# Small tiles padded so that every tile TensorE reads begins at the same place modulo 256 bytes

## The chip, the core and the metric

The kernel runs on one core of a Trainium2 chip. The core has a matrix engine (TensorE; PE in the profile, PEld for its weight loads), a vector engine (VectorE, DVE), an activation engine (ScalarE, ACT), GpSimd (POOL) and SyncE (SP, which here issues the weight DMAs). They share SBUF, a memory of 128 partitions, and run on their own, held together by semaphores; TensorE reads SBUF and writes its sums to PSUM. The metric is the device time of one launch in microseconds: the median of three runs is 2596.28 us (2596.21 to 2597.89).

## The reference

Two small transformers in a row, over 512 tokens of 1024 features, all in float32. The first has a latent attention, a squared-ReLU feed-forward, a differential attention and a second such feed-forward, each followed by a layer norm of `alpha * x + m`. The second has a forgetting attention, a SwiGLU, a retention and a second SwiGLU, each behind an RMS norm and added to `x`.

```python
def first_block(x, ...):
    for i in range(2):
        m = _mla(x, ...) if i == 0 else _diff_attn(x, ...)
        x = _layernorm(ALPHA * x + m, ln_mix_g[i], ln_mix_b[i])
        x = _layernorm(ALPHA * x + square(relu(x @ ffn_w_up[i])) @ ffn_w_down[i],
                       ln_ffn_g[i], ln_ffn_b[i])
    return x

def second_block(x, ...):
    for i in range(2):
        h = rmsnorm(x, norm_mix[i])
        x = x + (forgetting_attention(h, ...) if i == 0 else retention(h, ...))
        h = rmsnorm(x, norm_ffn[i])
        gu = h @ ffn_w_in[i]
        x = x + (silu(gu[..., :D_FF_2]) * gu[..., D_FF_2:]) @ ffn_w_out[i]
    return rmsnorm(x, final_norm)
```

The feed-forwards are 1024 to 4096 to 1024 in the first block and 1024 to 2 x 2816, then 2816 to 1024, in the second.

## The kernel before

Everything stays in SBUF: the stream `X` as four tiles of 128 tokens by 1024 features, and its transpose, features on partitions, in two parts `XH` and `XL`. float32 products are made of float32r ones: each operand is split into a high part and what is left of it (`split`, lines 113 to 120: ScalarE rounds, VectorE subtracts), and each product is three matmuls, high by high, high by low and low by high (`mm3`, lines 148 to 153; lines 150, 151 and 152 are the three). Weights come from HBM in chunks of 512 KB (128 partitions by 1024 numbers) into the two tiles `raw`, and are split into the rings `whi` and `wlo` of five tiles each.

There are eight stages: `mla`, `f0`, `diff`, `f1`, `fox`, `g0`, `ret`, `g1` (four attentions, each followed by its feed-forward). Two forms of product carry nearly all the time:

- `fgemm` (line 160): a 128-column piece of the weights is the stationary operand, the one that TensorE loads ahead; `XH` or `XL` with 512 tokens is the moving one, streamed through. In the profile these are `ps<-XH,whi` and so on (the projections in the up half of a feed-forward, the gates of the retention) and `pj<-XH,whi` (query and key projections). The first four tiles behind a norm run in halves of 256 tokens (`fhead`, line 168).
- `mm_t` (line 204): 128 tokens of the activations are stationary, 512 columns of the weights move. These are `ta`, `tb<-whi,jh` (the down half of a feed-forward, whose hidden activations `h` or `z` are split into `jh` and `jl` just ahead), `v<-whi,XH` (values) and `ta`, `tb<-whi,VH` (output projections).

TensorE loads the stationary operand of the next matmul while the present one streams, so two reads of SBUF run beside each other. Attention scores of one query tile (`s`), the softmax on the other engines, the transposes of its result (`pt`) and the product with the values (`o`) are woven into projections that fill TensorE's time: `PLAN` says how many filler products go with a query tile (`n`), and how much of TensorE's work in ns (`ln`, `sm`, `pv`, ...) is put before something that waits for a chain of the other engines. That work is counted in `tick` (line 131) as columns at 2.4 GHz, not measured.

SBUF is given out by pools, one after the other; a tile begins where the tile ahead of it ends, rounded up to 32 bytes per partition. So a small tile moves the begin of all that lie behind it. The places of the built program, modulo 256 bytes, are these (all matmul operands are cut from their tiles in steps of 512 or 2048 bytes, so a cut has its tile's place; the one exception is the 32-column weight of the forget gates):

| tiles | before | with the change |
|---|---|---|
| `X`, `XH`, `XL`, `idn` (the identity), `mask` | 128 | 128 |
| `raw`, `whi`, `wlo`, all stages | 224 | 128 |
| `CH`, `KH`, `qkh`, `PH` and their low parts in `mla` | 224 | 128 |
| `jh`, `jl` in `f0`, `f1`; `VH`, `VL` in `diff`, `fox` | 224 | 128 |
| `jh`, `jl` in `g0`, `g1`; all operands of `ret` (`H`, `L`, `VH`, `AH`, `zj`, `jh`, `yn`) | 96 | 128 |
| `qa`, `ka`, `kl` in `diff` | 64 | 128 |
| `PH`, `PL`, `e0`, `e1`, `sq` in `diff` | 160 | 128 |
| `qkh`, `qkl`, `ck`, `ch`, `PH`, `PL`, `e` in `fox` | 192 | 128 |

The tiles that cause this are `mh` (4 numbers) and `col` (16), line 55; the 24 small tiles of line 71; `ss` in `rms_fin` (2 numbers, four of them, line 345); `nlam`, `sub` and `ones` in `diff` (line 736); `s1` there (4 numbers, three buffers, line 793); and `bf` and `rc` in `fox` (line 856). A program prints the functions:

Of the kernel before, what the change touches and what calls it, by code (L numbers as in the profile page):

```python
# [9 lines left out]
F32 = mybir.dt.float32  # L10
# [5 lines left out]
PSUM = bass.MemoryType.PSUM  # L16
# [3 lines left out]
NT = 4  # L20
# [8 lines left out]
AUTO = True  # L29
# how much of the tensor engine's other work (ns) is put before what waits for a chain of the  # L30
# other engines, and how many products of that work go with each query tile
PLAN = {
# [8 lines left out]
class Net:  # L41
    def __init__(self, ctx, tc, A):
        self.tc, self.nc, self.A = tc, tc.nc, A
        nc = self.nc
        self.cst = ctx.enter_context(tc.tile_pool(name="cst", bufs=1))
        self.wp = ctx.enter_context(tc.tile_pool(name="wp", bufs=1))
        self.sm = ctx.enter_context(tc.tile_pool(name="sm", bufs=1))
        self.pp = ctx.enter_context(tc.tile_pool(name="pp", bufs=8, space=PSUM))
        c = self.cst
        self.X = c.tile([128, NT, D], F32, name="X")  # L50
        self.XH = c.tile([128, 8, S], F32R, name="XH")
        self.XL = c.tile([128, 8, S], F32R, name="XL")
        self.idn = c.tile([128, 128], F32, name="idn")
        self.mask = c.tile([128, S], F32, name="mask")
        self.mh = c.tile([128, 4], F32, name="mh")
        self.col = c.tile([128, 16], F32, name="col")
        self.seq = []
        self.n_dma = self.n_split = self.n_get = self.n_done = 0
        self.raw, self.sp = {}, {}
        self.fq = []  # L60
        self.unit = 0
        self.rt = self.tables = None
        self.late = {}
        self.owed = 0
        self.clk, self.dq, self.busy = 0.0, [], False
# [4 lines left out]
    def small(self, n, name):  # L70
        return self.sm.tile([128, 8], F32, tag="small", name=name, bufs=24)[:, 0:n]

    # weight stream: every chunk is [128, n] of float32, split into two float32r parts
    def dma_next(self, eng=None):
# [46 lines left out]

    # work behind a chain of the other engines is issued only after enough of the tensor
    # engine's other work: clk counts what the tensor engine was given, in ns
    def defer(self, delay, fn):
# [33 lines left out]

    # features on partitions: out[m, tok] over kts k-tiles, weights stationary
    def fgemm(self, ps, w, off, kts, xh, xl, n0=0, n1=S, m=128):  # L160
# [5 lines left out]

    # the first tiles after a norm run in token halves, so that the norm's tail is hidden
    def fhead(self, n, evac):
# [35 lines left out]
    def mm_t(self, ps, t, lh, ll, w, first, last):  # L204
        # two k-tiles of a [128 tok, 512] product
        ts = slice(t * 128, t * 128 + 128)
        for j in range(2):
            ws = slice(j * 512, j * 512 + 512)
            self.mm3(ps, lh[:, j, ts], ll[:, j, ts], w[0][:, ws], w[1][:, ws], first and j == 0, last and j == 1)

    # tokens on partitions: out[tok, 1024] in two column halves, lhs(c) -> (hi, lo) [128, 2, 512]
    def t_first(self, nch, lhs, fin0, ahead=True):
# [69 lines left out]

    # one 512-column half of a normed [128, 1024] token tile into xT
    def to_xT(self, src, t, g):
# [56 lines left out]
    def rms_fin(self, pool, g, dst=None):  # L341
        nc = self.nc
        X = [self.halves(self.X[:, t, :]) for t in range(NT)]
        G = self.halves(g)
        ss = [pool.tile([128, 2], F32, name=f"ss{t}", bufs=1) for t in range(NT)]
        out = {}

        def add(t, h, ps):
            nc.vector.tensor_tensor(X[t][h], X[t][h], ps, op=ALU.add)
            tmp = pool.tile([128, 512], F32, tag="ntmp", name="ntmp", bufs=self.plan.get("nb", 4))  # L350
            nc.scalar.activation(tmp, X[t][h], AF.Square, accum_out=ss[t][:, h:h + 1])

        def a(t, ps):
            add(t, 1, ps)
            rs = self.rms_scale(ss[t], D)
            for h in range(2):
                tmp = pool.tile([128, 512], F32, tag="ntmp", name="nt2", bufs=self.plan.get("nb", 4))
                nc.vector.scalar_tensor_tensor(tmp, X[t][h], rs, G[h], op0=ALU.mult, op1=ALU.mult)
                if dst is not None:
                    nc.sync.dma_start(out=dst[t * 128:t * 128 + 128, h * 512:h * 512 + 512], in_=tmp)  # L360
                out[t, h] = tmp

        def fb(t):
            for h in range(2):
                self.to_xT(out.pop((t, h)), t, h)

        return lambda t, ps: add(t, 0, ps), a, (fb if dst is None else lambda t: None), True
# [10 lines left out]

    # causal softmax numerators of [128 q, keys] in PSUM; sum into rs
    def softmax(self, pool, s, qt, tag, sm, scale=1.0):  # L380
# [22 lines left out]

    # out^T [dv, q] = sum over keys of V^T P^T; V is [tok, head, (tile, dv)], and the result takes
    # the place of its head's values as [dv, head, (tile, q)]
    def pv(self, VH, VL, h, PH, PL):
# [6 lines left out]

    # heads cut into query tiles: scores of one tile, other work for the tensor engine, and the
    # transposes and values behind the chains of the softmax
    def attend(self, pool, heads, scores, VH, VL, post, fills):
# [25 lines left out]

    # rotary embedding with features on partitions; swap names, in each group of 32 partitions, the
    # partner of a feature
    def rope(self, pool, src, swap, C, Sn):
# [8 lines left out]

    # cos and signed sin of positions * inv, features on partitions
    def rope_tables(self, pool, tmp, which, tags=("t0", "t1", "t2"), bufs=1):
# [212 lines left out]

    # attention, its output projection and the norm behind it  # L670
    def attn_out(self, outer, p, scores, VH, VL, nready, post, fills, gname, bname, row):
# [42 lines left out]

    # one 512-column half of a token-major projection: 4 chunks of two k-tiles
    def v_half(self, VH, VL, dst):
# [11 lines left out]
    def diff(self):  # L728
        nc, A, tc = self.nc, self.A, self.tc
        mm = nc.tensor.matmul  # L730
        with ExitStack() as outer:
# [3 lines left out]
            p = outer.enter_context(tc.tile_pool(name="d_a", bufs=1))  # L735
            nlam = p.tile([128, 1], F32, name="nlam")
            sub = p.tile([128, 1], F32, name="sub")
            ones = p.tile([128, 2], F32, name="ones")
            with tc.tile_pool(name="d_0", bufs=1) as p0:
# [15 lines left out]
            p = outer.enter_context(tc.tile_pool(name="d_b", bufs=1))  # L755
            qk, ready, s1 = {}, set(), {}

            def evac(h, which):
                def f(ps):
                    r = self.rope(p, ps, DIFF_SWAP, C, Sn)  # L760
                    # a sub-head's queries lie above their low parts, its keys twice: one product of full
                    # height gives two of the three parts
                    if which == 0:
                        qk[h] = [p.tile([128, 2, S], F32R, tag=n, name=n, bufs=2) for n in ("qa", "ka")]
                        qk[h].append(p.tile([128, S], F32R, tag="kl", name="kl", bufs=2))
                    q, k, kl = qk[h]
                    for i in range(2):
                        own, other = slice(64 * i, 64 * i + 64), slice(64 - 64 * i, 128 - 64 * i)
# [19 lines left out]
            def scores(h, qt):  # L788
# [3 lines left out]
                if qt == 0:  # L792
                    s1[h] = p.tile([128, 4], F32, tag="s1", name="s1", bufs=3)
                q, k, kl = qk[h]
                ss = [self.ps("s") for _ in range(2)]
# [17 lines left out]
            def post(h, o):  # L813
# [6 lines left out]
                def sums():  # L820
# [5 lines left out]
                    nc.vector.tensor_copy(s8, sps[:, 0:8])  # L826
                    # the values lack the division by the sum of the first softmax; so does eps
                    nc.vector.tensor_tensor(rr, s1[h], s1[h], op=ALU.mult)
# [19 lines left out]
    def fox(self):  # L848
        nc, A, tc = self.nc, self.A, self.tc
        mm = nc.tensor.matmul  # L850
        with ExitStack() as outer:
# [3 lines left out]
            pa = p = outer.enter_context(tc.tile_pool(name="x_a", bufs=1))  # L855
            bf = p.tile([32, 1], F32, name="bf")
            nc.gpsimd.dma_start(out=bf, in_=A["fox_b"])
            rc = p.tile([32, 16], F32, name="rc")
            nc.gpsimd.dma_start(out=rc, in_=A["c_rows"])
# [282 lines left out]
def pack_v(w):  # L1142
    # 512 columns, two k-tiles a chunk
    return w.reshape(-1, 2, 128, 512).transpose(0, 2, 1, 3).reshape(-1, 128, 1024)


def pack_h(w):
    # two 512-column halves, each in chunks of two k-tiles
    return np.concatenate([pack_v(np.ascontiguousarray(w[:, :512])), pack_v(np.ascontiguousarray(w[:, 512:]))])


# rotary features of the latent attention, the two halves side by side in each group of 32
ROPE_ORDER = np.array([16 * (i // 32) + i % 16 + 32 * (i % 32 // 16) for i in range(64)])
# [110 lines left out]
```

## Time and profile before

| | |
|---|---|
| median of three runs | 2596.28 us (2596.21 to 2597.89) |
| profiled execution, first to last instruction | 2594.1 us |
| outside that span, against the median | 2.2 us |
| TensorE busy, granted clock | 2561.4 us (99%), 0.998 of full speed |
| VectorE, ScalarE, GpSimd busy | 1289.7 us (50%), 929.4 us (36%), 170.4 us (7%) |
| DMA | 233.05 MB, mean 90 GB/s |

Matmuls are pipelined: the profile models each one's end, so that its shown duration (some 390 ns at 512 columns) overlaps the next. What counts for the time is the pitch, the distance from one matmul's start to the next one's start. It is read from the start times of a timeline, or from a row that gives the first and the last start and the count of a group.

### The profile page before, as it was taken

Reading aid. Unit: us, or ns where it says so; the run is one execution under the profiler, and the core shown is the slowest. Engines: PE = TensorE matmul, PEld = TensorE weight load, DVE = VectorE, ACT = ScalarE, POOL = GpSimd, SP = SyncE. Lnnn points to the kernel's source line nnn. Section 1 sums busy time; section 2 is a strip of 40 time slices with the busy share of each in tenths; the row PEclk is TensorE's granted clock in tenths of the full one; section 3 lists DMA queues with packets and bytes.
Section 4 is the critical chain, followed back from the end, with each engine's and each line's share of the span. In section 5 each row is a group of like instructions: output and inputs, shape, how many; then the busy total and the mean of one; then the engine's idle time right before and its main releaser. Section 6 shows DMA issues by size and latency. Waiting matters only on the chain.

```text
span 2594.1 us, 30292 instructions
## 1 busy us (share of the span) xinstructions
PE 2561.4 (99%) x12164; PEld 2100.7 (81%) x12164; DVE 1289.7 (50%) x1961; ACT 929.4 (36%) x1416; POOL 170.4 (7%) x238
## 2 busy tenths in 40 slices
PE   8999999999999999999999999999999999999998
PEld 7778888887778888887778888888888888888887
DVE  6865334566986333546455432244455544432243
ACT  5634223335663323334443322233322233322232
POOL 1100000012431000003000000000000000000000
PEclk9999999999999999999999999999999999999999
DMA  4213323323122322232211322222322222322322
GB/s 153 98 49 126 98 90 98 98 76 98 58 65 90 98 98 90 98 98 84 74 57 49 119 93 97 90 96 91 112 77 85 77 82 81 106 98 90 98 90 74
DMA packets 65837, 233.05 MB, mean 90 GB/s; under 512 B 7536, under 2 KB 7680, under 8 KB 65696
## 3 DMA queue, kind: packets, MB, share of 16 engines
q1 hardware_dynamic: 62064, 219.21, 25.8%
q0 software_dynamic: 3488, 11.55, 1.4%
q8 instruction: 95, 1.56, 0.3%
q14 instruction: 46, 0.38, 0.0%
q10 hardware_dynamic: 144, 0.36, 0.0%
HBM read 228.99 MB, written 2.10 MB: 89 GB/s over the span
## 4 chain that ended last, share of the span: by engine, by line
PE 54%; POOL 0%; issue 0%; ACT 0%; DVE 0%; DVEq 0%; POOLq 0%; ACTq 0%
PE ps L151 8%; PE ps L152 8%; PE ps L150 8%; PE ta L150 2%; PE ta L152 2%; PE ta L151 2%; PE tb L152 2%; PE tb L151 2%; PE tb L150 2%; PE pj L150 2%; PE v L150 2%; PE v L152 2%; PE pj L152 2%; PE pj L151 2%; PE v L151 2%; PE tp L156 1%
## 5 line engine op out<-in xcount | busy, mean ns | idle before, releaser
L117 DVE TENSOR_TENSOR wlo<-raw,whi 128x1024 fp32r<-128x1024 f32 (+2 forms) x415 | 507.6, 1225 | 535.1 <-ACT whi L116 530.5
L116 ACT CAST whi<-raw 128x1024 fp32r<-128x1024 f32 (+2 forms) x415 | 431.4, 1041 | 878.2 <-PE ps L151 578.5
L150 PE MATMUL ps<-XH,whi 128*128 128x512 f32 (+1 forms) x1664 | 609.7, 367 | 2.1 <-ACT XH L116 2.1
L151 PE MATMUL ps<-XL,whi 128*128 128x512 f32 (+1 forms) x1664 | 608.8, 366 | 0.2 <-DVE XL L117 0.2
L152 PE MATMUL ps<-XH,wlo 128*128 128x512 f32 (+1 forms) x1664 | 608.5, 366 | 0.0
L150 PEld LDWEIGHTS ps<-XH,whi 128*128 128x128 f32 x1664 | 314.2, 189 | 57.7 <-ACT XH L116 2.3
L151 PEld LDWEIGHTS ps<-XL,whi 128*128 128x128 f32 x1664 | 314.4, 189 | 56.0 <-DVE XL L117 0.7
L152 PEld LDWEIGHTS ps<-XH,wlo 128*128 128x128 f32 x1664 | 314.3, 189 | 55.8
L150 PE MATMUL ta<-whi,jh 128*128 128x512 f32 x496 | 194.6, 392 | 0.0
L152 PE MATMUL ta<-whi,jl 128*128 128x512 f32 x496 | 194.3, 392 | 0.0
L151 PE MATMUL ta<-wlo,jh 128*128 128x512 f32 x496 | 194.3, 392 | 0.0
L150 PE MATMUL tb<-whi,jh 128*128 128x512 f32 x448 | 176.5, 394 | 0.0
L152 PE MATMUL tb<-whi,jl 128*128 128x512 f32 x448 | 175.6, 392 | 0.0
L151 PE MATMUL tb<-wlo,jh 128*128 128x512 f32 x448 | 175.6, 392 | 0.0
L117 DVE TENSOR_TENSOR jl<-h,jh 128x1024 fp32r<-128x1024 f32 x64 | 78.4, 1225 | 174.8 <-ACT jh L116 174.8
L116 ACT CAST jh<-h 128x1024 fp32r<-128x1024 f32 x64 | 67.6, 1056 | 205.7 <-PE ta L151 110.8
L150 PE MATMUL pj<-XH,whi 128*128 128x512 f32 x288 | 121.2, 421 | 0.0
L152 PE MATMUL pj<-XH,wlo 128*128 128x512 f32 x288 | 114.3, 397 | 0.0
L151 PE MATMUL pj<-XL,whi 128*128 128x512 f32 x288 | 113.8, 395 | 0.0
L152 PEld LDWEIGHTS ta<-whi,jl 128*128 128x128 f32 x496 | 93.3, 188 | 20.6
L151 PEld LDWEIGHTS ta<-wlo,jh 128*128 128x128 f32 x496 | 93.3, 188 | 20.3
L150 PEld LDWEIGHTS ta<-whi,jh 128*128 128x128 f32 x496 | 93.3, 188 | 20.3
(325 smaller groups left out, 3612.2 us busy)
## 6 DMA issues: line engine op xcount, KB each, us to landing
raw<-in_w_in SPq DMA_DIRECT2D x88, 512.0 KB, 3.3
raw<-in_w_up SPq DMA_DIRECT2D x64, 512.0 KB, 3.3
raw<-in_w_dn SPq DMA_DIRECT2D x64, 512.0 KB, 3.3
raw<-in_w_r SPq DMA_DIRECT2D x48, 512.0 KB, 3.3
raw<-in_w_out SPq DMA_DIRECT2D x44, 512.0 KB, 3.3
raw<-in_w_d SPq DMA_DIRECT2D x24, 512.0 KB, 3.3
raw<-in_w_x SPq DMA_DIRECT2D x24, 512.0 KB, 3.3
raw<-in_w_ro SPq DMA_DIRECT2D x16, 512.0 KB, 3.3
```

The lines of the kernel that those rows point to most:

```text
L116: nc.scalar.copy(hi, src)
L117: (eng or nc.vector).tensor_tensor(lo, src, hi.bitcast(F32), op=ALU.subtract)
L150: mm(ps, ah, bh, start=first, stop=False)
L151: mm(ps, ah, bl, start=False, stop=False)
L152: mm(ps, al, bh, start=False, stop=last)
L156: self.nc.tensor.transpose(out, src, self.idn)
```

## The change

It alters sizes and places of small tiles alone. `mh` and `col` become cuts of one tile of 64 numbers (256 bytes), `nlam`, `sub` and `ones` in `diff` and `bf` and `rc` in `fox` likewise; each `ss` gets 16 numbers (four of them are 256 bytes); `s1` moves from the stage's pool to the pool of the small tiles, with 8 numbers (32 bytes) each, and the ring of that pool shrinks from 24 to 21, so that both together are 24 times 32 bytes. Comments are gone too. After it every operand of a matmul lies as the table's last column says.

```diff
-        self.mh = c.tile([128, 4], F32, name="mh")
-        self.col = c.tile([128, 16], F32, name="col")
+        mc = c.tile([128, 64], F32, name="mc")
+        self.mh, self.col = mc[:, 0:4], mc[:, 16:32]
...
-        return self.sm.tile([128, 8], F32, tag="small", name=name, bufs=24)[:, 0:n]
+        return self.sm.tile([128, 8], F32, tag="small", name=name, bufs=21)[:, 0:n]
...
-        ss = [pool.tile([128, 2], F32, name=f"ss{t}", bufs=1) for t in range(NT)]
+        ss = [pool.tile([128, 16], F32, name=f"ss{t}", bufs=1) for t in range(NT)]
...
-            nlam = p.tile([128, 1], F32, name="nlam")
-            sub = p.tile([128, 1], F32, name="sub")
-            ones = p.tile([128, 2], F32, name="ones")
+            few = p.tile([128, 64], F32, name="few")
+            nlam, sub, ones = few[:, 0:1], few[:, 8:9], few[:, 16:18]
...
-                    s1[h] = p.tile([128, 4], F32, tag="s1", name="s1", bufs=3)
+                    s1[h] = self.sm.tile([128, 8], F32, tag="s1", name="s1", bufs=3)[:, 0:4]
...
-            bf = p.tile([32, 1], F32, name="bf")
+            few = p.tile([32, 64], F32, name="few")
+            bf, rc = few[:, 0:1], few[:, 16:32]
             nc.gpsimd.dma_start(out=bf, in_=A["fox_b"])
-            rc = p.tile([32, 16], F32, name="rc")
```

Names and buffer numbers apart, each engine has the same instructions in the same order before and after. What differs beside the places is which buffers of the smaller ring are used again, and with that a few semaphores waited for. GpSimd has the only two waits that are new in number: at the layer norm of `mla` the rows of line 269 for the third and the fourth token tile wait for ScalarE beside VectorE, since an earlier reader of theirs on ScalarE had the buffer. On VectorE two waits for GpSimd stand at neighbouring rows of a softmax in `fox`; TensorE's and ScalarE's waits are the same.

## Rows read from the trace of the kernel before

**Rows 1.** The page: span, engines' busy time, granted clock in 40 slices, chain's shares.

```profile
span 2594.1 us, 30292 instructions
...
PE 2561.4 (99%) x12164; PEld 2100.7 (81%) x12164; DVE 1289.7 (50%) x1961; ACT 929.4 (36%) x1416; POOL 170.4 (7%) x238
...
PEclk9999999999999999999999999999999999999999
...
PE 54%; POOL 0%; issue 0%; ACT 0%; DVE 0%; DVEq 0%; POOLq 0%; ACTq 0%
```

**Rows 2.** Tile view of jh in f0's down half: durations, first and last start.

```profile
L150 PE MATMUL ta<-whi,jh x125: 389/389/389, 382.8 to 467.1; 128*128 128x512 f32 x125
```

**Rows 3.** Tile view of jh in g0's down half.

```profile
L150 PE MATMUL ta<-whi,jh x86: 390/393/404, 1679.6 to 1738.9; 128*128 128x512 f32 x86
```

**Rows 4.** Tile view of XH in the up halves of f0 and g0.

```profile
L152 PE MATMUL ps<-XH,wlo x221: 392/397/400, 223.8 to 378.4; 128*128 128x512 f32 x111
...
L152 PE MATMUL ps<-XH,wlo x318: 392/397/400, 1453.8 to 1676.6; 128*128 128x512 f32 x159
```

**Rows 5.** Tile view of XH: the values in ret, the 256-token halves in diff.

```profile
L150 PE MATMUL v<-whi,XH x29: 392/392/392, 1827.9 to 1847.5; 128*128 128x512 f32 x29
...
L150 PE MATMUL ps<-XH,whi x40: 277/281/283, 567.8 to 581.7; 128*128 128x256 f32 x40
```

**Rows 6.** Timeline of PE in mla, 23 projection matmuls: start us, us, line, out<-in.

```profile
50.14 0.39 PE L151 MATMUL pj<-CL,whi 128*128 128x512 f32 x1
...
55.13 0.39 PE L152 MATMUL pj<-KH,wlo 128*128 128x512 f32 x1
```

**Rows 7.** Timeline of PE in ret, retained scores by values.

```profile
1902.35 0.39 PE L150 MATMUL y<-VH,AH 128*128 128x512 f32 x1
...
1903.05 0.39 PE L150 MATMUL y<-VH,AH 128*128 128x512 f32 x1
1903.27 0.39 PE L151 MATMUL y<-VL,AH 128*128 128x512 f32 x1
1903.50 0.39 PE L152 MATMUL y<-VH,AL 128*128 128x512 f32 x1
1903.72 0.39 PE L150 MATMUL y<-VH,AH 128*128 128x512 f32 x1
```

**Rows 8.** Timeline of PE in mla's attention, 256-wide scores.

```profile
63.02 0.28 PE L150 MATMUL s<-qkh 128*128 128x256 f32 x1
...
63.37 0.28 PE L652 MATMUL s<-kph,qp 128*128 128x256 f32 x1
```

**Rows 9.** Groups of PE by form, whole span: xcount, busy us, mean ns, idle before.

```profile
L150 PE MATMUL ps<-XH,whi 128*128 128x512 f32 x1216 | 482.2, 397 | 0.0
...
L150 PE MATMUL ta<-whi,jh 128*128 128x512 f32 x496 | 194.6, 392 | 0.0
...
L150 PE MATMUL tb<-whi,jh 128*128 128x512 f32 x448 | 176.5, 394 | 0.0
...
L150 PE MATMUL ps<-XH,whi 128*128 128x256 f32 x448 | 127.5, 285 | 2.1 <-ACT XH L116 2.1
...
L150 PE MATMUL pj<-XH,whi 128*128 128x512 f32 x288 | 121.2, 421 | 0.0
...
L150 PE MATMUL v<-whi,XH 128*128 128x512 f32 x256 | 102.6, 401 | 2.0 <-DVE VL L117 2.0
...
L156 PE MATMUL pt<-idn,e 128*128 128x128 f32 x240 | 43.0, 280 | 7.0 <-DVE e L808 7.0
...
L150 PE MATMUL tb<-whi,zj 128*128 128x512 f32 x48 | 18.9, 394 | 0.0
```

**Rows 10.** Busy us by engine: stages diff and g0.

```profile
core 0: us, PE busy (x) PEld busy (x) DVE busy (x) ACT busy (x) POOL busy (x), PEclk, DMA share, GB/s
557.00:819.00 262.00, 248.44 (x1298) 198.78 (x1298) 204.34 (x472) 133.99 (x281) 81.26 (x64) 1.00 0.21 67
1429.00:1803.00 374.00, 374.00 (x1716) 306.57 (x1715) 136.83 (x135) 112.11 (x135) 4.36 (x13) 1.00 0.29 95
```

## The prediction

> **What bounds the kernel.** First the page: TensorE is busy 2561.4 of 2594.1 us, at a granted clock of nine tenths or more in every slice, which is the 2.4 GHz level; the chain that ended last is TensorE in all shares that are not zero [rows 1]. VectorE has 50%, ScalarE 36%, so in the large stages the time is the number of matmuls times their pitch. In g0 TensorE is busy all 374.00 us, VectorE 136.83 and the DMA 0.29 of its time [rows 10].
>
> Second the pitch, from first and last start and count of a group that repeats every three matmuls. In f0's down half it is (467.1 - 382.8) / 124 / 3 = 226.6 ns, and no matmul differs from another (389/389/389) [rows 2]. g0's down half is the same code with the same shapes, and its pitch is (1738.9 - 1679.6) / 85 / 3 = 232.5 ns, with durations that scatter from 390 to 404 [rows 3]. By the table of places, what differs is that `whi` and `jh` both begin at 224 modulo 256 in f0, and at 224 and 96 in g0. The up halves, `XH` at 128 and `whi` at 224, have 154.6 / 220 / 3 = 234.2 and 222.8 / 317 / 3 = 234.3 ns [rows 4]; the values, `whi` 224 and `XH` 128, 19.6 / 28 / 3 = 233.3 ns [rows 5]. 512 columns at 2.4 GHz are 213.3 ns, so some 13 ns are lost at equal places and 19 to 21 at unequal ones.
>
> Two more rows say that equality is what matters, not the form of product or the place itself. In mla weights are stationary and activations move, as in the up halves, but both at 224: 22 pitches take 55.13 - 50.14 = 4.99 us, 226.8 ns [rows 6]. In ret both are at 96: the first three pitches after a change of work take 0.70 us, and the next three 0.67, or 223 to 227 ns with the rounding of the starts [rows 7]. So a stream at equal places falls into the short pitch after some matmuls; I count six without gain after each break, twice what rows 7 show.
>
> **What the change does, part by part.** All operands come to 128, so I put the pitch of every long 512-column stream at 226.7 ns. Counts are three times those of one line [rows 9].
>
> - `ps`, 1216 x 3 = 3648 matmuls at 234.3. The 16 gate tiles of ret stand alone between scores, 24 matmuls each, and lose 16 x 6 = 96 to the transient. 3552 x 7.6 ns = 27.0 us.
> - `jh`, `zj` at 96: 496 + 448 - 512 (f0 and f1, equal already: 2 layers x 2 halves x 16 chunks x 8) + 48 = 480, times 3 = 1440; some 40 fall to transients. 1400 x 5.8 = 8.1 us.
> - `v<-whi,XH`, 256 x 3 = 768, of which 192 in pieces of 21 to 30 keep three quarters: 720 x 6.6 = 4.8 us.
> - `pj<-XH`, 288 x 3 = 864. In ret 288 in pieces of 21 to 33 keep four fifths; in diff and fox 576 in pieces of about 12 keep half. 518 x 7.6 = 3.9 us.
> - mla's output projection from `XH`, 192, not all in a row: 0.8 us.
>
> Together 44.6 us. What does not count: the 256-token halves, 448 x 3 = 1344 matmuls at (581.7 - 567.8) / 39 / 3 = 118.8 ns with `XH` and `whi` at unequal places [rows 5, 9]. Nothing long shows this width at equal places. The nearest are scores of mla, all at 224: 0.35 us over three pitches, 117 ns [rows 8], which would be 2.4 us. If half of a 512-column matmul's loss stayed, 106.7 + 6.7 = 113.4 ns, it would be 7.3 us; at the longest of the ordinary durations, 283 for 281, they would be 2 ns slower, 2.7 us. I take nothing, as the short row is not told from 118.8 by its rounding. The transposes `pt` and the 320- and 384-wide products of mla's start, which waits for its loads, get nothing.
>
> The engines that split, add and normalise have tiles at new places too; no row shows them otherwise, and where TensorE sets the end even a few per cent of 136.83 us in 374 stay covered [rows 10]. The two added waits on GpSimd are for ScalarE work that ended softmaxes earlier, a norm later nothing waits for; had they a price it would be once one chain of about 0.5 us. The ring of 21 instead of 24 small tiles is seven query tiles deep at three tiles each. Instruction order is the same.
>
> What is late next: the chains behind TensorE's own work. A norm waits behind 5500 to 8500 counted ns, some 33 matmuls of 213 ns at `ln` 7000; these now pass 33 x 7.6 = 0.25 us sooner. At eight norms that is 2.0 us at most if each chain is only just covered. In diff VectorE is busy 204.34 of 262 us and TensorE idles 7.0 us there for `e` before `pt` [rows 9, 10]; of the 2 us that diff's values and projections save, perhaps half comes back as such waits. I take 1.6 off both together. The net is 44.6 - 1.6 = 43 us.
>
> The profiled execution would have a span of 2594.1 - 43 = 2551.1 us. It stands 2.2 us under the median of 2596.28, and so the forecast of the median is 2553.3 us.
>
> **The Trainium skill on this.** The difference between rows 2 and 3 has the weight load and the stream disturb each other. The page "TensorE: Matmul & The Clock Gate", section "Step-by-step: what each phase is for", says that the stream and the weight load have independent read ports of SBUF; by that alone places could not matter and the time would stay at 2596.3 us. Here the trace does not agree: 226.6 and 232.5 ns for the same code. This is the second rival below. The page "SBUF — State Buffer", section "Door 1: The DMA port swizzle (why `[64,N]` ≈ `[32,N]`)", gives lines of 16 bytes, of which every place in both kernels is a multiple; by it 128 is as good as 224 or 96, and the sum stands. No run here has yet shown a long stream with both at 128.
>
> **The rivals.**
>
> - *Only products with moving weights gain.* The long aligned streams in the trace are down halves; weights-stationary ones have only the 22 pitches of rows 6 for them. If the up halves and projections keep 234.3 for a reason of their own (say the eight tiles of `XH` against one weight tile), 8.1 + 4.8 + 0.8 = 13.7 us are left less 1.0 for norms: 2583.6 us. Against it stand rows 6.
> - *Places do not decide at all.* g0 and f0 differ in the function ahead of the products and the hidden tile as well, and the streams of other engines run beside them. Then nothing moves: 2596.3 us. Against it: `v` in ret and `ps` in f0 have neither in common, and all three unequal pairs of places are slow.
> - *The place itself decides, and 128 is a bad one* (slower). Both equal places that are seen short, 224 and 96, are 32 modulo 64; no long stream has both operands at a multiple of 64. If a stream from a multiple of 64 meets the weight load as the unequal ones do, the aligned streams of now lose the short pitch: 512 x 3 = 1536 matmuls of f0 and f1 and some 500 of output projections, values times scores and mla. 2000 x 7.6 = 15 us, while the others stay: 2611.5 us. It decides if f0's down half rises over 230 ns. For it speaks only that 128 is untried.
> - *128 is a better one.* A start at a multiple of 64 might save a further part of the 13 ns that equal places still lose. Half of it, 6.7 ns, over some 8700 matmuls in long streams would be 58 us more: 2495 us. Nothing in the trace speaks for it but the size of what is left.
>
> **How the numbers follow.** The forecast gets 0.76, with a range of its own of 2542 to 2565: below, the 7.3 us of the 256-token halves and 4 us if transients are as short as in rows 7; above, 12 us if breaks keep the breaks' pitch longer and the chains take what they can. Gain in moving weights alone or another part of it, 2566 to 2590: 0.10. Nothing: 0.04. Slower: 0.06. Better place: 0.04. A range of 2541 to 2576 leaves out the better place, part of the partial case, none and slower, 0.18 in all. A change under 0.2% (5.2 us) is what a measurement of this kernel can't tell from none. Faster 0.76 + 0.10 + 0.04 = 0.90, within 0.2% 0.04, slower 0.06.
>
> **What would show it.** Tile views of the same groups: `ps<-XH` in f0 and g0, `jh` in g0 and `v` in ret at pitches of 226 to 227 ns with durations of 389 alone; `jh` in f0 unchanged. The up half of f0, 672 matmuls, would be 5.1 us shorter, that of g0, 960, 7.3 us; diff and fox together under 5 us. Wrong would be any long stream over 230 ns, or idle time of TensorE that grows by more than 3 us.

## The result, and the profile after

Measured: a median of 2553.45 us in 4 runs (2552.55 to 2555.57) against 2596.69 for the kernel before in 4 runs beside it. The ratio is 0.9834, with a 95% interval of 0.982 to 0.9848. The forecast was 2553.3. The profiled execution took 2555.57 us, and its span is 40.3 us shorter than before's.

The page of the changed kernel, in the rows that answer [rows 1]:

```profile
span 2553.8 us, 30294 instructions
...
PE 2520.0 (99%) x12164; PEld 2099.9 (82%) x12164; DVE 1289.7 (51%) x1961; ACT 928.9 (36%) x1416; POOL 169.3 (7%) x238
...
PEclk9999999999999999999999999999999999999999
...
PE 54%; POOL 0%; issue 0%; ACT 0%; DVE 0%; DVEq 0%; POOLq 0%; ACTq 0%
```

The same 12164 matmuls, and the others' busy times as before: TensorE's own 2561.4 us became 2520.0. The tile views of the changed kernel: f0's down half, its up half, the up half and the down half of g0, ret's values, diff's 256-token halves (durations min/median/max in ns, first and last start in us):

```profile
L150 PE MATMUL ta<-whi,jh x125: 389/389/389, 376.9 to 461.3; 128*128 128x512 f32 x125
...
L152 PE MATMUL ps<-XH,wlo x221: 389/389/389, 223.0 to 372.6; 128*128 128x512 f32 x111
...
L152 PE MATMUL ps<-XH,wlo x316: 389/389/389, 1442.2 to 1656.4; 128*128 128x512 f32 x158
...
L150 PE MATMUL ta<-whi,jh x86: 389/389/389, 1660.7 to 1718.5; 128*128 128x512 f32 x86
...
L150 PE MATMUL v<-whi,XH x29: 389/389/395, 1806.3 to 1825.4; 128*128 128x512 f32 x29
...
L152 PE MATMUL ps<-XH,wlo x40: 283/283/283, 561.9 to 576.0; 128*128 128x256 f32 x40
```

Where scattered durations stood (392/397/400 in [rows 4], 390/393/404 in [rows 3]) there is one number, 389, as always in [rows 2]. The pitches, worked as in the prediction, are 226.7 ns in the up halves (149.6 / 220 / 3 and 214.2 / 315 / 3) for 234.2, 57.8 / 85 / 3 = 226.7 in g0's down half for 232.5, 227.4 for the values, and 226.9 in f0's down half (84.4 / 124 / 3; the row's times are rounded to 0.1 us), as before. The last row went the other way: 14.1 / 39 / 3 = 120.5 ns for 118.8 in [rows 5].

Since instruction order is the same, each matmul's start-to-start time can be compared with its own of before. Summed by group, where "at waits" means behind a wait or at TensorE's lower clock:

| group | matmuls | before ns | after ns | us | predicted us |
|---|---|---|---|---|---|
| `ps`, 512 columns | 3644 | 234.26 | 226.82 | -27.1 | -27.0 |
| stationary `jh`, `jl`, `zj` | 2959 | 229.48 | 226.78 | -8.0 | -8.1 |
| `v`, in streams | 792 | 233.02 | 227.33 | -4.5 | -4.8 |
| `v`, at waits | 24 | 415.2 | 481.7 | +1.6 | (in chains) |
| `pj`, in streams | 908 | 233.10 | 229.31 | -3.4 | -3.9 |
| output projections `ta`, `tb` | 524 | | | -0.8 | -0.8 |
| 256-token halves, in streams | 1300 | 118.64 | 119.84 | +1.6 | 0 |
| the same at waits | 44 | 223.8 | 248.1 | +1.1 | (in chains) |

What is left of the 40.3 us is some 0.8 us, spread over scores, transposes and small waits. By stage the spans fell by 4.95 us in f0, 5.07 in f1, 9.75 in g0, 8.43 in ret, 10.09 in g1, 0.95 in mla and 1.20 in fox; diff took 0.1 us longer.

Why diff gained nothing in this execution is seen behind its values. The timeline of PE there (start us, us, line, tiles, idle time before), then the windows of the same place, both of the changed kernel:

```profile
605.09 0.80 PE L150 MATMUL v<-whi,XH 128*128 128x512 f32 x1 [2.22 <-DVE VL L117]
605.68 0.63 PE L151 MATMUL v<-wlo,XH 128*128 128x512 f32 x1
606.11 0.63 PE L152 MATMUL v<-whi,XL 128*128 128x512 f32 x1
...
608.74 0.39 PE L150 MATMUL v<-whi,XH 128*128 128x512 f32 x1
608.96 0.39 PE L151 MATMUL v<-wlo,XH 128*128 128x512 f32 x1
```

```profile
599.00:602.40 3.40, 3.40 (x18) 2.73 (x17) 0.90 (x1) 0.27 (x1) 0.00 (x0) 1.00 0.71 199
602.40:605.80 3.40, 1.18 (x5) 0.66 (x4) 2.59 (x4) 3.40 (x6) 0.00 (x0) 0.86 0.41 142
605.80:609.00 3.20, 3.20 (x11) 2.49 (x10) 3.13 (x10) 1.15 (x5) 0.00 (x0) 0.61 0.32 129
```

The columns are those of [rows 10]; the last but two is the granted clock. TensorE waits 2.22 us for `VL`, and behind it the granted clock falls, to a mean of 0.61 in the last window: the pitch is 0.43 us, the 1.2 GHz level. From 605.09 to 608.96 ten pitches take 3.87 us. In a later profile of the same changed kernel (the one beside the five norms below) the clock stayed at 1.00 there, and the same ten take 2.41 us, from 605.93 to 608.34. So the fall costs 1.5 us; the rest of the table's 1.6 is the longer wait. In the kernel before this wait was 2.02 us and the granted clock stayed at 1.00. The length of the wait does not decide by itself: in that later profile it was 2.75 us, with no fall behind it, and diff took 0.8 us less than before.

The 1.1 us of the 256-token halves is the clock too, in the main. At the norm into fox both kernels have a granted clock of 0.50 for 6.8 us in all, before from 1173.1 to 1176.5 and from 1183.4 to 1186.8 us, after from 1171.5 to 1178.3. Before, the first of these stretches fell on the norm's transposes and the products ahead of the halves; after, the whole fell on the halves, and 27 of them in place of 16 ran at the lower clock.

### The profile page after: what moved, and what is told of

Its sections match the earlier page's. It is cut to its first block, busy times and chain, and to the rows that moved or that the text cites. A ratio compares the mean times of both kernels' runs of the same rounds, so it can differ in the third digit from the quotient of the medians.

```text
span 2553.8 us, 30294 instructions
## 1 busy us (share of the span) xinstructions
PE 2520.0 (99%) x12164; PEld 2099.9 (82%) x12164; DVE 1289.7 (51%) x1961; ACT 928.9 (36%) x1416; POOL 169.3 (7%) x238
## 4 chain that ended last, share of the span: by engine, by line
PE 54%; POOL 0%; issue 0%; ACT 0%; DVE 0%; DVEq 0%; POOLq 0%; ACTq 0%
PE ps L150 8%; PE ps L151 8%; PE ps L152 8%; PE ta L150 2%; PE ta L152 2%; PE tb L152 2%; PE ta L151 2%; PE tb L150 2%; PE tb L151 2%; PE pj L150 2%; PE v L150 2%; PE pj L152 2%; PE pj L151 2%; PE v L152 2%; PE v L151 2%; PE tp L156 1%
## 5 line engine op out<-in xcount | busy, mean ns | idle before, releaser
L150 PE MATMUL ps<-XH,whi 128*128 128x512 f32 (+1 forms) x1664 | 602.4, 362 | 2.3 <-ACT XH L116 2.3
L151 PE MATMUL ps<-XL,whi 128*128 128x512 f32 (+1 forms) x1664 | 601.4, 361 | 0.0
L152 PE MATMUL ps<-XH,wlo 128*128 128x512 f32 (+1 forms) x1664 | 601.1, 361 | 0.0
```

Source lines behind the costliest of these rows:

```text
L150: mm(ps, ah, bh, start=first, stop=False)
L151: mm(ps, ah, bl, start=False, stop=False)
L152: mm(ps, al, bh, start=False, stop=last)
```

## Experiments

**Every operand at 0 instead of 128.** The shared tile of constants is cut to 32 numbers and put ahead of `X`.

```diff
+        mc = c.tile([128, 32], F32, name="mc")
+        self.mh, self.col = mc[:, 0:4], mc[:, 16:32]
...
-        mc = c.tile([128, 64], F32, name="mc")
-        self.mh, self.col = mc[:, 0:4], mc[:, 16:32]
```

> Every operand of TensorE begins at 0 modulo 256 instead of 128 (the 128 bytes of the shared constants stand first). Theory A, the difference of places decides and not the place: the up half of f0, the down half of g0 and the values of ret have pitches of 226 to 227 ns, the 256-token halves 120 to 121, and the time is that of the changed kernel, 2553 us within 0.2%. Rival B, the place itself decides (all places that were seen short, 224, 96 and 128, are not multiples of 256): long streams leave 226.7 by more than 2 ns, to either side, and the time moves by more than 15 us.

Measured: 2556.0 us (2555.23 to 2557.23), ratio 0.9842 (0.9825 to 0.9858). The tile views of g0's up and down halves in this kernel:

```profile
L152 PE MATMUL ps<-XH,wlo x317: 389/389/389, 1441.9 to 1656.8; 128*128 128x512 f32 x159
...
L151 PE MATMUL ta<-wlo,jh x86: 389/389/389, 1660.6 to 1718.4; 128*128 128x512 f32 x86
```

Again 226.7 ns (214.9 / 316 / 3 and 57.8 / 85 / 3). A common place of 0, 128 or 224 gives the same pitch: neither rival that spoke of the place itself holds. By the tiles' sizes `whi` begins an odd multiple of 256 bytes behind `XH` in the changed kernel, and an even one here, where the tile of constants no longer stands between them: 256 bytes apart is as good as equal.

**How near must the places be?** The ring of weights is made one tile, and each of its five slots begins some bytes further than the last, against `XH` at a fixed place: steps of 32 bytes from 0, the same from 128, and 0, 4, 8, 16, 32 bytes.

```diff
+SHIFT = (0, 8, 16, 24, 32)
...
-        hi = self.wp.tile([128, 1024], F32R, tag="whi", name="whi", bufs=RING)
-        lo = self.wp.tile([128, 1024], F32R, tag="wlo", name="wlo", bufs=RING)
+        if i == 0:
+            self.ring = self.wp.tile([128, 2048 * RING + 32], F32R, name="whi", bufs=1)
+        o = i % RING * 2048 + SHIFT[i % RING]
+        hi, lo = self.ring[:, o:o + 1024], self.ring[:, o + 1024:o + 2048]
...
```

> The five ring slots of the weights begin at 0, 32, 64, 96 and 128 modulo 256, high and low part of a slot alike; XH, XL and all else at 128. Theory A: in the up halves the slot at 128 has 226.7 ns after some matmuls, that at 32 (difference 96) about 234, that at 0 (difference 128) about 232, and those at 64 and 96 are new; no slot is shorter than 226.7, and the span lies between 2575 and 2590 us. Rival C, what shortens the pitch is one common place for all slots, so that successive matmuls repeat the same pattern: then no slot has 226.7 and the span is 2594 or more. Rival B: the slots follow their place whatever XH has, so that the one at 0 or 64 may be short.

> The same with slots at 128, 160, 192, 224 and 0 (17 small tiles in their ring, so that all else stays at 128). Theory A: 226.7 ns at 128, 234 at 224, 232 at 0 (128 apart), 160 and 192 new, none under 226.7; span between 2575 and 2590 us. Rival C: no slot at 226.7. If the sign of the difference did not matter, 160 would be like 96 and 192 like 64 in the other sweep.

> Slots 0, 4, 8, 16 and 32 bytes behind 128. How near to equal must the places be? Theory A1, a line of 16 bytes is what counts: 4 and 8 behave as 0 (226.7 ns), 16 and 32 do not (230 or more). Theory A2, coarser, lines of 64: all five 226.7. Theory A3, exact: only the slot with 0 has 226.7. Span 2553 to 2590 us by that.

Measured: 2593.87, 2593.76 and 2595.33 us, one run each. Mean pitch in ns by the place of the next stationary operand less that of the moving one, modulo 256 bytes, over matmuls with at least eight like them ahead (280 to 490 for each of the 512-wide; from start times):

| less | `ps`, 512 wide | 256 wide |
|---|---|---|
| 0 | 226.7 | 120.0 |
| 4 | 232.2 | 118.3 |
| 8 | 230.9 | 115.5 |
| 16 | 233.0 | 118.3 |
| 32, 64 | 233.3 | 118.3, 115.8 |
| 96 | 234.3 | 118.2 to 118.6 |
| 128 | 232.8 to 233.2 | 118.7 |
| 160 | 233.6 | 119.9 |
| 192 | 228.9 | 117.0 |
| 224 | 233.3 | 117.5 |

In down halves, where the weights move, it is 226.7 ns at 0, 237.0 at 252, 233.3 at 248, 231.7 at 240 and 229.1 at 192. The timeline of PE in the third sweep shows a chunk at equal places and, from 1504.9 us on, the next one, 4 bytes off:

```profile
1501.93 0.39 PE L155 MATMUL ps<-XH,whi 128*128 128x512 f32 x1
...
1504.19 0.39 PE L153 MATMUL ps<-XH,whi 128*128 128x512 f32 x1
...
1506.51 0.39 PE L154 MATMUL ps<-XL,whi 128*128 128x512 f32 x1
...
1510.00 0.39 PE L154 MATMUL ps<-XL,whi 128*128 128x512 f32 x1
```

Ten pitches in 2.26 us, 226 ns, and fifteen in 3.49 us, 232.7. Of the steps tried, which go down to one number of 4 bytes, only equality is short; 4 bytes cost nearly all. The page "SBUF — State Buffer" of the Trainium skill, section "Door 1: The DMA port swizzle (why `[64,N]` ≈ `[32,N]`)", gives lines of 16 bytes; with 16 bytes as long as 4, such a line does not explain this loss. The slot at equal places is short among four that are not, so one common place for all slots is not needed. The table also gives back pitches of the kernel before: 96 is its up halves (234.3), 160 its values (233.3) and 128 g0's down half (232.5).

The times missed what was expected, 2575 to 2590 us for the first two. One slot in five gained: the up halves took 11.4, 7.2 and 11.1 us less than before. But f0's and f1's down halves, at equal places before, lost them in four slots of five and took 8.3, 7.2 and 9.2 us more, which the expectations had left out.

**Are other engines or the DMA in it?** The kernel before, with weights from the 32nd chunk on neither loaded nor split; the ring's five pairs are used again.

```diff
+QUIET = 31
...
+        if i >= QUIET:
+            self.sp[i] = self.slot[i % RING]
+            self.n_split += 1
+            return
...
```

> The kernel before, with no weights loaded or split from the sixth chunk of f0 on: the five ring slots are used again and again, so the computation is wrong there, and the DMA queue, ScalarE and VectorE fall still in the long up halves but for the squares. Theory A, the two reads of TensorE itself meet: pitches stay as before, 234.3 ns in the up halves, 226.7 in f0's down half, 232.4 in g0's, 233.3 for values; span 2585 to 2595 us, as a few waits go. Rival D, the streams of the other engines (which write and read the same rings) meet TensorE's: the up halves fall to 227 ns or below, and the span by 20 us or more.

Measured: 2593.68 us. Windows of f0's and g0's up halves in this kernel, and the tile view of the first:

```profile
230.00:370.00 140.00, 140.00 (x599) 112.57 (x598) 24.01 (x37) 17.97 (x29) 0.54 (x1) 1.00 0.01 3
1460.00:1660.00 200.00, 200.00 (x855) 160.80 (x854) 16.05 (x21) 13.91 (x21) 0.00 (x0) 1.00 0.00 1
```

```profile
L157 PE MATMUL ps<-XH,wlo x200: 392/397/400, 229.8 to 369.6; 128*128 128x512 f32 x100
```

The DMA share is 0.01 where the kernel before has this:

```profile
230.00:370.00 140.00, 140.00 (x600) 112.53 (x599) 52.40 (x62) 41.65 (x54) 0.54 (x1) 1.00 0.30 96
```

VectorE and ScalarE do less than half, and the pitch is still 139.8 / 199 / 3 = 234.2 ns. In g0, where VectorE is busy 8% of the time, it is 234.3, and the down halves and the values keep their pitches of before too, as expected of theory A. So the other engines and the DMA do not make the loss; together with the sweeps, in which the places of TensorE's two operands set it, that leaves TensorE's own reads. The page "TensorE: Matmul & The Clock Gate" of the Trainium skill, section "Step-by-step: what each phase is for", has the next weights loaded through a port of their own, which takes nothing from the running matmul. These runs differ: the same code has 226.7 or 228.9 to 237.0 ns by the places alone.

**Which pair counts?** Only the low weights stand 128 bytes off.

```diff
+        o = i % RING * 1024
+        hi, lo = self.ring[:, o:o + 1024], self.ring[:, 1024 * RING + 32 + o:1024 * RING + 32 + o + 1024]
...
```

> The changed kernel with the low weights 128 bytes off, high weights at the place of XH (17 small tiles in their ring). Which load meets which stream? If the load for the next matmul beside the present stream counts, in the up halves the matmul of line 151 (behind which the low weights are loaded) gets long, by some 6 to 17 ns, and line 152 and 150 stay shorter; if a matmul's own weights counted, it would be line 152. In the down halves, where the low weights move, it is line 151 that streams them. If the pattern runs on over all three, all have 229 to 233. Span 2565 to 2592 us.

Measured: 2584.29 us. Of this kernel's up halves, the timeline of PE; its lines 152, 153, 154 are 150, 151, 152 of the others, and the third uses the low weights:

```profile
1500.53 0.39 PE L152 MATMUL ps<-XH,whi 128*128 128x512 f32 x1
1500.76 0.40 PE L153 MATMUL ps<-XL,whi 128*128 128x512 f32 x1
1500.99 0.40 PE L154 MATMUL ps<-XH,whi 128*128 128x512 f32 x1
1501.23 0.39 PE L152 MATMUL ps<-XH,whi 128*128 128x512 f32 x1
```

Over 1200 of each, the first has 226.8 ns, the second, beside which the low weights are loaded, 232.5, and the third 234.1. In down halves only the product that moves the low weights is long: 233.7 against 227.3 and 226.7. Its own stationary operand and the one loaded beside it have the same place there, so this row does not tell the two theories apart, and in up halves both the second and the third are long.

The first sweep tells them apart, at changes of chunk in its up halves (26 of each kind, from start times). Where a chunk at equal places is followed by one at 128, the last matmul of the old chunk uses weights at an equal place while unequal ones are loaded beside it: 232.5 ns. Where equal weights follow unequal ones at 224, the last matmul uses unequal weights while equal ones are loaded: 226.7. So it is the load beside the matmul that counts. Then the third product's 234.1 ns above is a loss that runs on from the second, which neither theory foresaw. It shows at changes of chunk as well: where equal weights follow ones at 128, in the second sweep, the last matmul has 229.3 ns, and the next two, whose own weights and loaded weights are both at equal places, still have 233.2 and 235.1.

**The two parts apart.** First the kernel before with the four sums of squares padded, and nothing else:

```diff
-        ss = [pool.tile([128, 2], F32, name=f"ss{t}", bufs=1) for t in range(NT)]
+        ss = [pool.tile([128, 16], F32, name=f"ss{t}", bufs=1) for t in range(NT)]
```

> One part alone: the kernel before with ss at 16 numbers, so that g0, g1 and ret have their own operands at 224 like the weights, and XH stays at 128. Theory A: jh in g0 and zj in ret fall from 232.4 to 226.7 ns, worth 8 us; up halves, values and projections stay; span 2586 us within 2.

Then the changed kernel with that and the two tiles `few` undone:

```diff
-        ss = [pool.tile([128, 16], F32, name=f"ss{t}", bufs=1) for t in range(NT)]
+        ss = [pool.tile([128, 2], F32, name=f"ss{t}", bufs=1) for t in range(NT)]
...
```

> The other parts alone: constants, small tiles, s1 and with them the weights at 128 like XH; ss, and the few of diff and fox, as before, so that jh in g0 and ret lie at 0 and those of f0 at 128. Theory A: up halves 226.7, values 226.7, g0's down half 232 to 233 (128 apart), f0's 226.7, the 256-token halves 120; span 2594.1 - 27.1 - 3.6 - 4.4 - 0.7 + 2.6 = 2561 us within 3.

Measured: 2588.01 and 2563.23 us, spans 2586.2 and 2561.5. g0's down and up halves, of the first and then of the second kernel:

```profile
L150 PE MATMUL ta<-whi,jh x86: 389/389/389, 1680.1 to 1737.9; 128*128 128x512 f32 x86
...
L150 PE MATMUL ps<-XH,whi x308: 392/397/400, 1453.8 to 1669.5; 128*128 128x512 f32 x154
```

```profile
L151 PE MATMUL ta<-wlo,jh x85: 390/393/404, 1660.7 to 1719.2; 128*128 128x512 f32 x85
...
L152 PE MATMUL ps<-XH,wlo x307: 389/389/389, 1441.9 to 1649.9; 128*128 128x512 f32 x154
```

Each part mends its own products: in the first kernel `jh` and `zj` behind fox give 7.9 us and `ps` keeps 234.3 ns, in the second `ps` gives 27.2 us and those keep 232.4. Against the profiled span of before they add: 2594.1 - 2586.2 = 7.9 and 2594.1 - 2561.5 = 32.6, together 40.5 for 40.3. That it meets within 0.2 us is luck, as the kernel before alone ran between 2595.61 and 2599.18 us.

**A version with the halves 8 bytes off.** The sweeps gave the 256-token halves 115.5 ns at 8 bytes. So the chunks behind seven norms, and later behind five, are put 8 bytes further in the ring, which takes some room from a ring of the norms.

```diff
+HEADS = {s + j for s in (26, 90, 122, 186, 219, 285, 349) for j in range(4)}
...
-    "f0": dict(ln=7000), "f1": dict(ln=8500), "g0": dict(ln=5500), "g1": dict(ln=5500),
+    "f0": dict(ln=7000, nb=3), "f1": dict(ln=8500, nb=3), "g0": dict(ln=5500), "g1": dict(ln=5500),
...
+        o = i % RING * (2048 + 64) + 2 * (i in HEADS)
```

> The changed kernel with the four weight chunks behind each of seven norms 8 bytes further on (slots 256 bytes apart for the room, three instead of four buffers for ntmp in f0 and f1): 256-token halves at a difference of 8, where the fine sweep had 115.5 ns, all other streams equal. Theory A: 1344 matmuls x (120.0 - 115.5) = 6.0 us less than the changed kernel, 2547 us; long streams 226.7. Rival E: the sweep's 115.5 comes from the slots beside it, and the halves stay at 118 to 120: 2553. Slower, if the smaller ntmp ring makes TensorE wait: over 2555, with idle time in the up halves.

> The changed kernel once more, as the measure for the run beside it on the same chip: 2553 us within 0.15%, 256-token halves at 120.0 ns. Whether TensorE's clock falls again for 3.4 us behind the wait for the values in diff is open; if it does not, diff is 1.5 us shorter than in its first profile.

> The 8 bytes only behind the five norms where the shorter halves came through in the run before (f0, f1, g0, ret, g1), the halves of diff and fox at equal places again, so that there TensorE does not come to the norm's chain and to the values sooner. Five stages at about 0.8 us: 4 us less than the changed kernel beside it, some 2551.5 us, 0.16%; waits of TensorE as in the changed kernel (2.0 to 2.8 us on the norm into fox, 2.2 to 2.7 on diff's values). If the difference stays under 2 us, the falls of the clock, which move by 1 to 3 us between runs, decide and not the halves.

> The changed kernel beside it on the same chip: 2555 us within 0.1%, 256-token halves near 120 ns.

Measured, each beside the changed kernel: seven norms 2554.16 us (2552.87 to 2556.13; ratio to before 0.982 to 0.9847) against 2555.80 (2553.36 to 2557.01; 0.9824 to 0.9851), five norms 2554.98 (0.9821 to 0.9848) against 2555.63 (0.9826 to 0.9853). Neither pair can be told apart; the 6.0 and 4 us that were expected did not come. The halves did get shorter, in diff's of the first version and of the changed kernel beside the second:

```profile
L155 PE MATMUL ps<-XH,whi x39: 277/278/278, 561.8 to 575.0; 128*128 128x256 f32 x39
```

```profile
L152 PE MATMUL ps<-XH,wlo x37: 283/284/284, 562.9 to 575.9; 128*128 128x256 f32 x37
```

13.2 / 38 / 3 = 115.8 ns for 13.0 / 36 / 3 = 120.4, and f0, f1, g0, ret and g1 were 0.6 to 0.8 us shorter each. It went back, in both versions, in a wait of the transposes for the norm into fox. Waits of PE (us in total, times, longest) in the version with five norms, and in the changed kernel beside it:

```profile
PE tp L159 <- ACT nt L335: 5.5, 3, 3.0
PE v L153 <- DVE VL L120: 3.0, 1, 3.0
```

```profile
PE tp L156 <- ACT nt L332: 2.8, 2, 2.0
...
PE v L150 <- DVE VL L117: 2.7, 1, 2.7
```

In this pair of profiles the clock takes back some as well: in the version it is granted at 0.50 from 605.7 to 609.1 and from 1172.3 to 1179.1 us, in the kernel beside it from 1171.1 to 1174.5 alone.

After the first version I took it that TensorE arrived too soon at the norm before fox. The second has fox's halves at equal places again and the same wait of 3.0 us: that reason falls. What both share is the ring of three for the norm's tiles. That it makes this wait is argued; no version that leaves this ring alone was tried.

## Why the prediction was right

- **The pitch at equal places.** All long 512-wide streams came to 226.7 to 227.4 ns, as read from [rows 2, 6]. It holds with weights stationary and weights moving, so the first rival falls; that places do not decide falls with it, and 128 is neither worse nor better than 0 or 224.
- **`ps`, `jh` and `zj`, the output projections.** Each within 0.2 us of its term. f0's up half and g0's gave most of their stages' 4.95 and 9.75 us, the rest of g0's being its down half.
- **`v` and `pj`.** 4.5 for 4.8 and 3.4 for 3.9 us; short pieces kept a little more of the break's pitch than the shares I gave them.
- **The 256-token halves** were the mis-sized term: I took nothing, and they lost 1.6 us in their streams, inside the bound of 2.7. The nearest value I had, 117 ns from scores with rounded starts in [rows 8], is not theirs at equal places, 120.0. At this width equal places are the longest of all those swept, with 160 next to them (119.9).
- **Chains, 1.6 us.** The size was near and the way it came was not. Waits for `e` before `pt` did not grow (7.0 to 6.9 us). What came back was mostly TensorE's clock, a term that the prediction does not have: 1.5 us behind the wait for `VL`, and most of the 1.1 us in fox's halves. The waits themselves grew by little, for `VL` from 2.0 to 2.2 us and of the transposes for a norm from 2.0 to 2.8. Such falls differ between executions: of the two later profiles of the changed kernel one has a fall at 607.5 us and the other none there. So that the chains came to their 1.6 us is luck.
- The sum of the terms, 44.6, was 2.4 us over what the streams gave together with the halves' loss, and the 2.2 us that I added from the profiled span to the median were 1.8 in this profiled execution, as in the others that list time and span; 2.2 set one execution's span against the median of others. Errors of a few us cancelled; that the forecast met the median within 0.2 us is partly luck. The mechanism, equal places and the short pitch in each stream, is not: it came out group by group.

What stays open: what in TensorE's two reads meets at unequal places, when a loss runs on, why 192 stands apart from 64, why 8 bytes suit the 256-wide products, and where the 13 ns that equal places still have over 213.3 come from.

## What to carry to other kernels

When a profile has one engine busy all the time, compare the pitch of equal shapes in different stages: two values for the same code are worth a look at where their operands begin. Here long 512-wide float32r products want the next stationary and the moving operand at the same place modulo 256 bytes, where 4 bytes off is as bad as most, and a padded small tile was all it took. Judge other widths by their own pitch, and expect waits and the clock behind them to take back a part.

## What the runs showed of the hardware

- In float32r, equal places give 226.67 ns for 512 columns and 120.0 ns for 256; 4 bytes off they are 232.2 (237.0 in down halves, with the sign turned) and 118.3.
- The loss belongs to the load beside the matmul (232.5 ns with equal weights in use and unequal ones loaded, 226.7 the other way round), and can run on into the next: 232.5 and 234.1 ns in up halves.
- It does not change when the DMA share goes from 0.30 to 0.01 (234.2 ns).
- A wait of 2.22 us was followed by a mean granted clock of 0.61, 1.5 us in cost; waits of 2.02 us (the kernel before) and 2.75 us (the changed kernel again) at the same place were not.
